# Two wide and narrow matmuls per weight tile become three narrow ones, and the sums are read straight from PSUM

## The chip, the core and the metric

The kernel runs on one core of a Trainium2 chip. TensorE does the matrix products into PSUM, VectorE (DVE), ScalarE (ACT) and GpSimd (POOL) the elementwise work, and the sync engine (SP) issues the loads. The metric is the device time of one execution in microseconds. Before the change it is 2220.55 us, the median of 3 runs that lie between 2220.05 and 2221.08.

## The reference

Two decoder layers over 256 tokens with 2048 features, all in float32. Each layer is a token mixer (latent attention with 8 heads beside retention with 8 heads, both fed by one product with `w_in`) and an MLP with squared ReLU:

```
h = rmsnorm(x, attn_norm[l])
proj = h @ w_in[l]                       # 2048 x 4928
c_q, c_kv, k_rope, rq, rk, rv, rg = jnp.split(proj, split_pts, axis=-1)
a = mla_attention(c_q, c_kv, k_rope, ...)     # w_uq, w_ukv
r = retention(rq, rk, rv, rg, cos128, sin128)
mixed = jnp.concatenate([rmsnorm(a, beta_attn[l]), r * beta_ret[l]], axis=-1)
x = x + mixed @ w_o[l]                   # 2048 x 2048
h = rmsnorm(x, mlp_norm[l])
x = x + jnp.square(jax.nn.relu(h @ w_up[l])) @ w_down[l]   # 2048 x 8192, 8192 x 2048
```

A final rmsnorm follows the last layer.

## The kernel before

**Split operands.** TensorE multiplies float32 data here in the kind float32r. To keep the result near float32, each operand is split into a head of few bits and the exact rest. `split` and `split_w` (L164 to L176) do it: ACT writes the head, DVE subtracts it and writes the rest. A product needs three parts: head by head, head by rest, rest by head.

**One weight tile, two matmuls.** A weight tile is 128 rows by 128 columns. Activations lie features by tokens, as `[128, 2, 256]`: the head's 256 tokens and then the rest's 256. `mac_feat` (L207) issues two matmuls for a weight tile. L209 loads the weight's head and streams all 512 activation columns, head and rest, into a whole PSUM bank. L210 loads the weight's rest and streams the 256 head columns into the bank's first half. So the second half holds one part of the sum and the first half the other two. `mac_tok` (L212) does the same with activations as the loaded side and weights as the streamed side (L214, L215); it serves the retention's values and the latent attention's values.

**The products.** `proj_feat` (L217) computes `nt` products side by side, 128 output features each, over 16 or 32 weight tiles in depth: `nt` is 2 in the token mixer, 4 in the MLP's first product (`UP_TILES`), and 4 or 2 in the output and second MLP products (`OUT_GROUPS`, `END_GROUPS`). Each product owns one of the 8 banks. `stream` (L196) loads 512 KB pieces of weights and splits them, ahead of use, into 6 buffers.

**The joins.** When a product is done, `join` (L225) adds the two halves: ACT copies the second half to SBUF (L227), DVE adds the first half to the copy (L228). `join_scaled` (L230) does so with a scale per token. What follows (squares, gates, ReLU, residual) reads the joined tile. In the MLP's first product it is a DVE operation that squares the ReLU (L643), then the split of the result for the next product.

**The key-value latent.** This product has 320 columns, streamed weights, and the form with three matmuls already (L349 to L351): the loaded tile of L349 and L350 is the same, but each of them loads it.

**Order.** The tile scheduler orders each engine's instructions from the program text, and places semaphore waits. Attention and retention work for the heads is woven between the pieces of the long products (`weave`, L181), in plain float32 matmuls.

Of the kernel before, what the change touches and what calls it, by code (L numbers as in the profile page):

```python
# [15 lines left out]
ALU = mybir.AluOpType  # L16
# [25 lines left out]
def two_pi_parts(scale, *bits):  # L42
    """2 * pi * scale as floats of few bits, whose products with whole numbers are exact, and one with the rest."""
    parts, rest = [], 2 * math.pi
    for n in bits:
        q = 2.0 ** (math.floor(math.log2(rest)) + 1 - n)
        parts.append(math.floor(rest / q) * q * scale)
        rest -= parts[-1] / scale
    return parts + [float(np.float32(rest * scale))]


# An angle is reduced by whole numbers of 2^15 turns, of turns, and of the turns that rounding has left; large parts
# first, while the differences are exact. Per number: turns, then (number, part) to subtract.
# [30 lines left out]
def kernel(ctx: ExitStack, tc: tile.TileContext, xt, positions, w_in, w_uq, w_ukv, w_o, w_up, w_down,  # L84
# [79 lines left out]
    def split(dst, src, scale=None):  # L164
        """dst[:, 0] = 12-bit head of src (times a column), dst[:, 1] = the exact rest."""
        head = dst[:, 0, :]
        if scale is None:
            nc.scalar.copy(head, src)  # L168
            nc.vector.tensor_tensor(dst[:, 1, :], src, head.bitcast(F32), op=ALU.subtract)  # L169
        else:  # L170
            nc.scalar.activation(head, src, AF.Copy, scale=scale)
            nc.vector.scalar_tensor_tensor(dst[:, 1, :], src, scale, head.bitcast(F32), op0=ALU.mult, op1=ALU.subtract)
# [5 lines left out]
    # Work that is woven into the long matrix products, a stage per four k-tiles.  # L178
# [17 lines left out]
    def stream(w, r0, c0, nk, width=256, kc=None):  # L196
        """Yields (k, split tile [P, 2, columns]) for rows r0.. and the columns from c0."""
        kc = kc or 1024 // width
        for s in range(0, nk, kc):
            raw = early.pop(0) if early else w_load(w[r0 + s * P:r0 + (s + kc) * P, c0:c0 + width], [P, kc, width])  # L200
            ws = w_tile([P, kc, 2, width])
            split_w(ws[:, :, 0, :], ws[:, :, 1, :], raw)
            for k in range(kc):
                yield s + k, ws[:, k]
            weave()

    def mac_feat(ps, wk, n0, act, first, last):  # L207
        """Features on partitions: ps[:, :256] + ps[:, 256:] accumulates wk.T @ act."""
        nc.tensor.matmul(ps, wk[:, 0, n0:n0 + P], act.rearrange("p s t -> p (s t)"), start=first, stop=False)  # L209
        nc.tensor.matmul(ps[:, 0:T], wk[:, 1, n0:n0 + P], act[:, 0, :], start=False, stop=last)  # L210

    def mac_tok(ps, wk, t0, act, first, last):  # L212
        """Tokens on partitions: ps[:, :256] + ps[:, 256:] accumulates act.T @ wk."""
        nc.tensor.matmul(ps, act[:, 0, t0:t0 + P], wk, start=first, stop=False)  # L214
        nc.tensor.matmul(ps[:, 0:256], act[:, 1, t0:t0 + P], wk[:, 0], start=False, stop=last)  # L215

    def proj_feat(w, r0, c0, acts, nt=2):  # L217
        ps = [bank() for _ in range(nt)]
        nk = len(acts)
        for k, wk in stream(w, r0, c0, nk, nt * P):  # L220
            for n in range(nt):
                mac_feat(ps[n], wk, n * P, acts[k], k == 0, k == nk - 1)
        return ps

    def join(ps, dst):  # L225
        tb = tmp("tb", 3)
        nc.scalar.copy(tb, ps[:, T:2 * T])  # L227
        nc.vector.tensor_tensor(dst, ps[:, 0:T], tb, op=ALU.add)  # L228

    def join_scaled(ps, dst, col):  # L230
        tb = tmp("tb", 3)
        nc.scalar.activation(tb, ps[:, T:2 * T], AF.Copy, scale=col)
        nc.vector.scalar_tensor_tensor(dst, ps[:, 0:T], col, tb, op0=ALU.mult, op1=ALU.add)

    def rope(ps, dst, cos, sin):
        t = tmp()
        join(ps, t)
        rotate(t, dst, cos, sin)
# [30 lines left out]
    def mean_squares(dst, accs, n, eps):  # L269
        """dst [P, 2] = mean square per token, tokens on partitions, plus eps (a number or a column)."""  # L270
        ps = abank()
        for t in range(2):
            for i, acc in enumerate(accs):
                nc.tensor.matmul(ps[:, t:t + 1], acc[:, t * P:(t + 1) * P], ones, start=i == 0, stop=i == len(accs) - 1)
        if isinstance(eps, float):
            nc.vector.tensor_scalar(dst, ps[:, 0:2], 1.0 / n, eps, op0=ALU.mult, op1=ALU.add)
        else:
            nc.vector.scalar_tensor_tensor(dst, ps[:, 0:2], 1.0 / n, eps, op0=ALU.mult, op1=ALU.add)

    def norm_col(accs, n):  # L280
        """1 / rms per token, tokens on partitions: [P, 2]."""
        v = col("nv")
        mean_squares(v, accs, n, EPS)
        return rsqrt(v, 2)

    def spread(c, tag=None):
        """Tokens from partitions to the free axis, the same on every partition."""
        ps = abank()
        for t in range(2):
            nc.tensor.matmul(ps[:, t * P:(t + 1) * P], c[:, t:t + 1].to_broadcast([P, P]), ident, start=True, stop=True)  # L290
        if tag is None:
            return ps[:, 0:T]
        d = cpool.tile([P, T], F32, tag=tag, name=tag)
        nc.scalar.copy(d, ps[:, 0:T])
        return d
# [5 lines left out]
    def norm_step(acc, tiles, j, g0):  # L301
        """Splits gain * x[j] and adds its squares."""
        xs = xpool.tile([P, 2, T], F32R, tag=f"xs{j}", name=f"xs{j}")
        split(xs, x[j], gcol(g0 + j))
        tiles.append(xs)
        if acc is not None:
            add_square(acc, x[j], j == 0)
# [11 lines left out]
    for l in range(DEPTH):  # L319
        g0 = l * G_LAYER  # L320
        # ================= token mixers =================
        with tc.tile_pool(name=f"mix{l}", bufs=1) as ap:
# [8 lines left out]
            # query latent  # L331
            acc_q = ap.tile([P, T], F32, tag="acccq", name="acccq")
            cq = []
            for c0 in range(COL_CQ, COL_CKV, 256):
                for ps in proj_feat(w_in[l], 0, c0, xs):
                    t = tmp()
                    join(ps, t)
                    add_square(acc_q, t, not cq)
                    s = ap.tile([P, 2, T], F32R, tag=f"cq{len(cq)}", name=f"cq{len(cq)}")
                    split(s, t, gcol(g0 + G_Q + len(cq)))  # L340
                    cq.append(s)

            # key-value latent and shared rotary key, tokens on partitions
# [21 lines left out]
            def scale_rows():  # L365
                # rs for x, and with rmsnorm(rs * c) = c * rsqrt(mean(c * c) + EPS / rs^2) the scales of the latents
# [22 lines left out]
                # feature-major again; the rotary key is kept twice and masked for the two heads of a pair  # L389
# [22 lines left out]
            def mla(i):  # L412
# [15 lines left out]
                for n in range(3):  # L428
                    ps = abank()
                    for k in range(4):  # L430
                        mac_feat(ps, wn[k] if n < 2 else wr[:, k], n * P if n < 2 else 0, cq[k], k == 0, k == 3)
                    if n < 2:
                        join(ps, qn[:, n, :])
                    else:
                        rope(ps, qr, tab[:, 1, 0, :], tab[:, 1, 1, :])
# [6 lines left out]
                for n in range(2):  # L442
                    ps = abank()
                    for k in range(2):
                        mac_feat(ps, wk[:, k], n * 256, ckv[k], k == 0, k == 1)
                    t = tmp()
                    join(ps, t)
                    nc.vector.tensor_tensor(kn[:, n, :], t, rows["tkvb"], op=ALU.mult)
                yield
                wvs = wk.rearrange("p k s (h u c) -> p k s h u c", h=2, u=2)[:, :, :, :, 1, :]  # L450
                for t_ in range(2):
                    ps = abank()
                    for k in range(2):
                        mac_tok(ps, wvs[:, k], t_ * P, ckv[k], k == 0, k == 1)
                    join_scaled(ps, v[:, t_, :], rows["tkv"][:, t_:t_ + 1])
# [51 lines left out]
            def ret_v(i):  # L507
                rv = two("rv")
                ps = [bank(), bank()]
                for k, wk in stream(w_in[l], 0, COL_RV + 256 * i, KD):  # L510
                    for t in range(2):
                        mac_tok(ps[t], wk, t * P, xs[k], k == 0, k == KD - 1)
                for t in range(2):
                    join_scaled(ps[t], rv[:, t, :], rows["rs"][:, t:t + 1])
# [49 lines left out]
            def ret_gate(i, res):  # L564
# [3 lines left out]
                for h, ps in enumerate(pss):  # L568
                    z, th = tmp(), tmp()
                    join(ps, z)  # L570
                    nc.vector.tensor_tensor(z, z, rows["rsb"], op=ALU.mult)
# [41 lines left out]
            for c0, nt in OUT_GROUPS:  # L613
                for n, ps in enumerate(proj_feat(w_o[l], 0, c0 * P, mixed, nt)):
                    j = c0 + n
                    t = tmp()
                    join(ps, t)
                    nc.vector.tensor_tensor(x[j], x[j], t, op=ALU.add)
                    norm_step(acc, ms, j, g0 + G_MLP)

        # ================= MLP =================
        with tc.tile_pool(name=f"mlp{l}", bufs=1) as up:
# [14 lines left out]
            for b in range(FF // FB):  # L637
                us = []
                for c in range(0, FB, UP_TILES * P):
                    for ps in proj_feat(w_up[l], 0, b * FB + c, ms, UP_TILES):  # L640
                        t = tmp()
                        join(ps, t)
                        nc.vector.scalar_tensor_tensor(t, t, 0.0, t, op0=ALU.max, op1=ALU.mult)  # L643
# [4 lines left out]
                for c0, nt in END_GROUPS if end else OUT_GROUPS:  # L648
                    for n, ps in enumerate(proj_feat(w_down[l], b * FB, c0 * P, us, nt)):
                        j = c0 + n  # L650
                        t = tmp()
                        join(ps, t)
                        nc.vector.tensor_tensor(t, t, rows["rs2b"], op=ALU.mult)
# [12 lines left out]
    # ================= final norm =================  # L666
# [36 lines left out]
```

## Time and profile before

| what | value |
|---|---|
| median of 3 runs | 2220.55 us (2220.05 to 2221.08) |
| span of the profiled execution | 2218.1 us |
| outside that span, against the median | 2.45 us |
| TensorE busy | 2191.8 us, 99% of the span |
| weight loads (PEld) busy | 1910.9 us, 86% |
| DVE busy | 1435.0 us, 65% |
| ACT busy | 1075.3 us, 48% |
| HBM traffic | 179 GB/s over the span |

The profiled execution's own time is its span and what lies around it; the median of the runs is 2.45 us longer than the span. Matmuls are pipelined: their lengths overlap, so the time of one is read from the distance between the starts of two neighbours, not from its length. Start times in a timeline are given to 0.01 us.

### The profile page before, as it was taken

The numbers are of one execution on the slowest core, as the hardware profiler recorded it, in microseconds if no ns is written. First come the engines' busy times: TensorE is split into PE (matmuls) and PEld (weight loads), VectorE is DVE, ScalarE is ACT, GpSimd is POOL, SyncE is SP. The second block draws the span as 40 slices with busy tenths as digits, with TensorE's granted clock in tenths as the row PEclk, the third lists the DMA queues.
The fourth block names the chain that finished last, engine by engine and source line by source line (L and its number), as shares of the span: only waits on it lengthen the run. The fifth ranks groups of instructions, "written<-read, shape, count | busy, mean of one in ns | idle before, by whom it ended". The sixth has DMA issues, their size and how long they took to land.

```text
span 2218.1 us, 32536 instructions
## 1 busy us (share of the span) xinstructions
PE 2191.8 (99%) x12552; PEld 1910.9 (86%) x12552; DVE 1435.0 (65%) x2494; ACT 1075.3 (48%) x1655; POOL 24.1 (1%) x34
## 2 busy tenths in 40 slices
PE   7999999999999999999999999999999999999997
PEld 6888888888888888888898888888888888888886
DVE  8878967656554556655668888666565555655564
ACT  7555545444444445444455554555453344444452
POOL 4000000000000000000000000000000000000000
PEclk9999999999999999999999999999999999999998
DMA  7556556666555666555655555566655556665553
GB/s 242 167 157 176 156 187 189 182 189 181 189 182 192 180 193 185 189 185 187 186 170 152 175 164 169 176 191 179 195 182 190 188 184 188 182 189 189 184 178 95
DMA packets 273115, 400.07 MB, mean 180 GB/s; under 512 B 12608, under 2 KB 143808, under 8 KB 272960
## 3 DMA queue, kind: packets, MB, share of 16 engines
q1 hardware_dynamic: 272000, 397.08, 57.9%
q8 instruction: 98, 1.61, 0.3%
q10 hardware_dynamic: 960, 0.92, 0.1%
q14 instruction: 57, 0.47, 0.1%
HBM read 395.85 MB, written 2.10 MB: 179 GB/s over the span
## 4 chain that ended last, share of the span: by engine, by line
PE 98%; DVE 1%; issue 0%; DMA 0%; ACT 0%; SPq 0%; DVEq 0%
PE mm L209 58%; PE mm L210 29%; PE mm L214 3%; PE mm L215 1%; PE at L209 1%; PE at L210 1%; PE at L466 0%; PE at L465 0%; PE mm L351 0%; PE mm L350 0%; PE mm L349 0%; PE at L214 0%; PE at L498 0%; PE at L527 0%; DMA raw<-w_in 0%
## 5 line engine op out<-in xcount | busy, mean ns | idle before, releaser
L176 DVE TENSOR_TENSOR w<-raw,w 128x1024 fp32r<-128x1024 f32 (+3 forms) x792 | 920.0, 1167 | 703.1 <-ACT w L175 702.3
L175 ACT CAST w<-raw 128x1024 fp32r<-128x1024 f32 (+3 forms) x792 | 792.7, 1005 | 919.8 <-PE mm L210 856.0
L209 PE MATMUL mm<-xs,w 128*128 128x512 f32 x2944 | 1048.2, 400 | 7.2 <-ACT w L175 7.2
L210 PE MATMUL mm<-xs,w 128*128 128x256 f32 x2944 | 827.1, 281 | 5.1 <-DVE w L176 5.1
L209 PE MATMUL mm<-u,w 128*128 128x512 f32 x2048 | 723.8, 399 | 0.0
L209 PEld LDWEIGHTS mm<-xs,w 128*128 128x128 f32 x2944 | 554.2, 188 | 141.0 <-ACT w L175 7.2
L210 PE MATMUL mm<-u,w 128*128 128x256 f32 x2048 | 575.3, 281 | 0.0
L210 PEld LDWEIGHTS mm<-xs,w 128*128 128x128 f32 x2944 | 557.4, 189 | 7.8 <-DVE w L176 7.6
L209 PEld LDWEIGHTS mm<-u,w 128*128 128x128 f32 x2048 | 384.9, 188 | 96.0
L210 PEld LDWEIGHTS mm<-u,w 128*128 128x128 f32 x2048 | 387.2, 189 | 0.0
L209 PE MATMUL mm<-mix,w 128*128 128x512 f32 x512 | 181.2, 399 | 0.0
L227 ACT COPY tb<-mm 128x256 f32<-128x256 f32 x280 | 100.6, 372 | 91.4 <-PE mm L210 87.4
L210 PE MATMUL mm<-mix,w 128*128 128x256 f32 x512 | 143.8, 281 | 0.0
L228 DVE TENSOR_TENSOR t<-mm,tb 128x256 f32<-128x256 f32 x280 | 107.9, 416 | 31.7 <-ACT tb L227 31.2
L209 PEld LDWEIGHTS mm<-mix,w 128*128 128x128 f32 x512 | 96.2, 188 | 23.9
L210 PEld LDWEIGHTS mm<-mix,w 128*128 128x128 f32 x512 | 96.8, 189 | 0.0
L214 PE MATMUL mm<-w,xs 128*128 128x512 f32 x256 | 92.5, 402 | 0.0
L215 PE MATMUL mm<-w,xs 128*128 128x256 f32 x256 | 71.5, 279 | 0.0
L168 ACT CAST u<-t 128x256 fp32r<-128x256 f32 x128 | 48.7, 405 | 27.4 <-DVE t L643 27.4
L214 PEld LDWEIGHTS mm<-w,xs 128*128 128x128 f32 x256 | 48.1, 188 | 10.5
L169 DVE TENSOR_TENSOR u<-t,u 128x256 fp32r<-128x256 f32 x128 | 48.9, 422 | 4.6 <-ACT u L168 0.7
L215 PEld LDWEIGHTS mm<-w,xs 128*128 128x128 f32 x256 | 48.3, 189 | 0.0
(167 smaller groups left out, 1102.2 us busy)
## 6 DMA issues: line engine op xcount, KB each, us to landing
raw<-w_up SPq DMA_DIRECT2D x256, 512.0 KB, 4.3
raw<-w_down SPq DMA_DIRECT2D x256, 512.0 KB, 3.7
raw<-w_in SPq DMA_DIRECT2D x144, 512.0 KB, 4.3
raw<-w_o SPq DMA_DIRECT2D x64, 512.0 KB, 4.3
raw<-w_uq SPq DMA_DIRECT2D x16, 384.0 KB, 3.9
raw<-w_in SPq DMA_DIRECT2D x16, 320.0 KB, 3.1
raw<-w_ukv SPq DMA_DIRECT2D x8, 512.0 KB, 4.2
x<-xt SPq DMA_DIRECT2D x8, 256.0 KB, 6.5
```

Source lines behind the costliest of these rows:

```text
L168: nc.scalar.copy(head, src)
L169: nc.vector.tensor_tensor(dst[:, 1, :], src, head.bitcast(F32), op=ALU.subtract)
L175: nc.scalar.copy(dst_h, src)
L176: nc.vector.tensor_tensor(dst_l, src, dst_h.bitcast(F32), op=ALU.subtract)
L209: nc.tensor.matmul(ps, wk[:, 0, n0:n0 + P], act.rearrange("p s t -> p (s t)"), start=first, stop=False)
L210: nc.tensor.matmul(ps[:, 0:T], wk[:, 1, n0:n0 + P], act[:, 0, :], start=False, stop=last)
L214: nc.tensor.matmul(ps, act[:, 0, t0:t0 + P], wk, start=first, stop=False)
L215: nc.tensor.matmul(ps[:, 0:256], act[:, 1, t0:t0 + P], wk[:, 0], start=False, stop=last)
L227: nc.scalar.copy(tb, ps[:, T:2 * T])
L228: nc.vector.tensor_tensor(dst, ps[:, 0:T], tb, op=ALU.add)
```

## The change

Each weight tile gets three matmuls of 256 columns, all into the same 256 columns of PSUM (`three`). Two products share a bank, one in each half (`halves`); only the first matmul of a bank carries the start flag. The sum of the three parts then stands in PSUM, so `join` and `join_scaled` are gone: consumers read PSUM, with a scale where `join_scaled` had one. The MLP's ReLU becomes an ACT operation that reads PSUM, and the square a DVE product of it with the PSUM sum.

```
+    def three(ps, lhs, rhs, start, stop):
+        nc.tensor.matmul(ps, lhs[0], rhs[0], start=start, stop=False, skip_group_check=True)
+        nc.tensor.matmul(ps, lhs[0], rhs[1], start=False, stop=False, skip_group_check=True)
+        nc.tensor.matmul(ps, lhs[1], rhs[0], start=False, stop=stop, skip_group_check=True)
     def mac_feat(ps, wk, n0, act, first, last):
-        nc.tensor.matmul(ps, wk[:, 0, n0:n0 + P], act.rearrange("p s t -> p (s t)"), start=first, stop=False)
-        nc.tensor.matmul(ps[:, 0:T], wk[:, 1, n0:n0 + P], act[:, 0, :], start=False, stop=last)
+        three(ps, [wk[:, s, n0:n0 + P] for s in range(2)], [act[:, s, :] for s in range(2)], first, last)
     def mac_tok(ps, wk, t0, act, first, last):
-        nc.tensor.matmul(ps, act[:, 0, t0:t0 + P], wk, start=first, stop=False)
-        nc.tensor.matmul(ps[:, 0:256], act[:, 1, t0:t0 + P], wk[:, 0], start=False, stop=last)
+        three(ps, [act[:, s, t0:t0 + P] for s in range(2)], [wk[:, s] for s in range(2)], first, last)
+    def halves(n):
+        out = []
+        for i in range(n):
+            if i % 2 == 0:
+                b = bank()
+            out.append(b[:, i % 2 * T:i % 2 * T + T])
+        return out
     def proj_feat(w, r0, c0, acts, nt=2):
-        ps = [bank() for _ in range(nt)]
+        ps = halves(nt)
...
-                mac_feat(ps[n], wk, n * P, acts[k], k == 0, k == nk - 1)
+                mac_feat(ps[n], wk, n * P, acts[k], k == 0 and n % 2 == 0, k == nk - 1)
-    def join(ps, dst):
-        tb = tmp("tb", 3)
-        nc.scalar.copy(tb, ps[:, T:2 * T])
-        nc.vector.tensor_tensor(dst, ps[:, 0:T], tb, op=ALU.add)
...
 -                        join(ps, t)
-                        nc.vector.scalar_tensor_tensor(t, t, 0.0, t, op0=ALU.max, op1=ALU.mult)
+                        nc.scalar.activation(t, ps, AF.Relu)
+                        nc.vector.tensor_tensor(t, t, ps, op=ALU.mult)
...
 -                        join(ps, t)
-                        nc.vector.tensor_tensor(t, t, rows["rs2b"], op=ALU.mult)
+                        nc.vector.tensor_tensor(t, ps, rows["rs2b"], op=ALU.mult)
```

The last two pieces are the MLP's first and second product. The other consumers (query latent, rotary, gate, output product, values) change in the same way.

On TensorE, in the MLP's first product, the eight matmuls of one step in depth for four output tiles stand in a row. `xs15` is the activation tile of that step, `w` the weight piece, `mm` the PSUM bank:

```order
L209 MATMUL mm_4165<-xs15_4154,w_4343 128x512
L210 MATMUL mm_4165<-xs15_4154,w_4343 128x256
L209 MATMUL mm_4166<-xs15_4154,w_4343 128x512
L210 MATMUL mm_4166<-xs15_4154,w_4343 128x256
L209 MATMUL mm_4167<-xs15_4154,w_4343 128x512
L210 MATMUL mm_4167<-xs15_4154,w_4343 128x256
L209 MATMUL mm_4168<-xs15_4154,w_4343 128x512
L210 MATMUL mm_4168<-xs15_4154,w_4343 128x256
```

After the change the same step has twelve matmuls, and two output tiles write to one `mm`:

```order
L210 MATMUL mm_10634<-xs15_4816,w_10841 128x256
L211 MATMUL mm_10634<-xs15_4816,w_10841 128x256
L212 MATMUL mm_10634<-xs15_4816,w_10841 128x256
L210 MATMUL mm_10634<-xs15_4816,w_10841 128x256
L211 MATMUL mm_10634<-xs15_4816,w_10841 128x256
L212 MATMUL mm_10634<-xs15_4816,w_10841 128x256
L210 MATMUL mm_10635<-xs15_4816,w_10841 128x256
L211 MATMUL mm_10635<-xs15_4816,w_10841 128x256
L212 MATMUL mm_10635<-xs15_4816,w_10841 128x256
L210 MATMUL mm_10635<-xs15_4816,w_10841 128x256
L211 MATMUL mm_10635<-xs15_4816,w_10841 128x256
L212 MATMUL mm_10635<-xs15_4816,w_10841 128x256
```

Each L209 of 512 columns has become an L210 and an L211 of 256 columns, each with its own weight load, and the old L210 is now L212; the number of columns stays 768 for a weight tile.

On DVE, at the end of the program, the last two products of the MLP are consumed. `rs2b` is the scale per token, `x_101` the last residual tile, `tb` the copied half, `nv` the start of the final norm:

```order
L228 TENSOR_TENSOR t<-mm,tb 128x256
L653 TENSOR_TENSOR t<-t,rs2b 128x256
L654 TENSOR_TENSOR x_101<-x_101,t 128x256
L253 TENSOR_TENSOR ssq<-ssq,sq 128x256
L228 TENSOR_TENSOR t<-mm,tb 128x256
L653 TENSOR_TENSOR t<-t,rs2b 128x256
L654 TENSOR_TENSOR x_101<-x_101,t 128x256
L276 TENSOR_SCALAR nv<-at 128x2
```

After the change the two additions of the halves are gone and the scaling reads PSUM:

```order
L649 TENSOR_TENSOR t<-mm,rs2b 128x256
L650 TENSOR_TENSOR x_101<-x_101,t 128x256
L257 TENSOR_TENSOR ssq<-ssq,sq 128x256
L649 TENSOR_TENSOR t<-mm,rs2b 128x256
L650 TENSOR_TENSOR x_101<-x_101,t 128x256
L280 TENSOR_SCALAR nv<-at 128x2
```

Nothing else moved there: the last operation before the final norm is still the residual's addition, two instructions (ACT's copy and DVE's addition) earlier in the chain.

## Rows read from the trace of the kernel before

**Rows 1.** The page: span, and busy time with share of each engine

```profile
span 2218.1 us, 32536 instructions
PE 2191.8 (99%) x12552; PEld 1910.9 (86%) x12552; DVE 1435.0 (65%) x2494; ACT 1075.3 (48%) x1655; POOL 24.1 (1%) x34
```

**Rows 2.** The page: lines of the chain that ended last

```profile
PE mm L209 58%; PE mm L210 29%; PE mm L214 3%; PE mm L215 1%; PE at L209 1%; PE at L210 1%; PE at L466 0%; PE at L465 0%; PE mm L351 0%; PE mm L350 0%; PE mm L349 0%; PE at L214 0%; PE at L498 0%; PE at L527 0%; DMA raw<-w_in 0%
```

**Rows 3.** All waits of TensorE: engine, line, releaser; us, times, longest

```profile
PE mm L209 <- ACT w L175: 7.2, 1, 7.2
PE mm L210 <- DVE w L176: 5.1, 4, 2.5
```

**Rows 4.** The page: costliest matmul groups, count, busy us, mean ns

```profile
L209 PE MATMUL mm<-xs,w 128*128 128x512 f32 x2944 | 1048.2, 400 | 7.2 <-ACT w L175 7.2
L209 PE MATMUL mm<-u,w 128*128 128x512 f32 x2048 | 723.8, 399 | 0.0
L209 PE MATMUL mm<-mix,w 128*128 128x512 f32 x512 | 181.2, 399 | 0.0
L214 PE MATMUL mm<-w,xs 128*128 128x512 f32 x256 | 92.5, 402 | 0.0
```

**Rows 5.** Timeline of TensorE in the MLP: start us, length us, instruction

```profile
1000.50 0.28 PE L210 MATMUL mm<-u,w 128*128 128x256 f32 x1
1000.61 0.40 PE L209 MATMUL mm<-u,w 128*128 128x512 f32 x1
...
1001.56 0.28 PE L210 MATMUL mm<-u,w 128*128 128x256 f32 x1
```

**Rows 6.** Stretch of the MLP: length, TensorE busy (instructions), clock, DMA

```profile
600.00:800.00 200.00, 200.00 (x1134) 1.00 0.58 185
```

**Rows 7.** Timeline of TensorE in the first token mixer

```profile
265.22 0.28 PE L210 MATMUL mm<-xs,w 128*128 128x256 f32 x1
265.34 0.39 PE L209 MATMUL mm<-xs,w 128*128 128x512 f32 x1
265.57 0.28 PE L210 MATMUL mm<-xs,w 128*128 128x256 f32 x1
...
266.26 0.28 PE L210 MATMUL mm<-xs,w 128*128 128x256 f32 x1
```

**Rows 8.** Timeline of TensorE in the key-value latent of layer 0

```profile
39.64 0.31 PE L349 MATMUL mm<-w,xs 128*128 128x320 f32 x1
...
47.56 0.31 PE L349 MATMUL mm<-w,xs 128*128 128x320 f32 x1
```

**Rows 9.** Timeline of TensorE: two L210 behind each other, twice

```profile
16.66 0.39 PE L210 MATMUL mm<-xs,w 128*128 128x256 f32 x1
16.89 0.28 PE L210 MATMUL mm<-xs,w 128*128 128x256 f32 x1
...
22.23 0.39 PE L210 MATMUL mm<-xs,w 128*128 128x256 f32 x1 [2.48 <-DVE w L176]
22.46 0.28 PE L210 MATMUL mm<-xs,w 128*128 128x256 f32 x1
```

**Rows 10.** Timeline of TensorE's weight loads there

```profile
22.34 0.19 PEld L210 LDWEIGHTS mm<-xs,w 128*128 128x128 f32 x1
```

**Rows 11.** Timeline of TensorE, two transposes of the latent attention

```profile
107.40 0.38 PE L489 MATMUL at<-cst,pr 128*128 128x128 f32 x2
```

**Rows 12.** TensorE by form, that transpose alone: count, busy us, mean ns

```profile
L489 PE MATMUL at<-cst,pr 128*128 128x128 f32 x48 | 7.9, 273 | 0.0
```

**Rows 13.** Timeline of the last product's consumers

```profile
2202.10 0.37 ACT L227 COPY tb<-mm 128x256 f32<-128x256 f32 x1 [8.57 <-PE mm L210]
...
2202.96 0.42 DVE L653 TENSOR_TENSOR t<-t,rs2b 128x256 f32<-128x256 f32 x1
```

**Rows 14.** The page: the joins' two groups

```profile
L227 ACT COPY tb<-mm 128x256 f32<-128x256 f32 x280 | 100.6, 372 | 91.4 <-PE mm L210 87.4
L228 DVE TENSOR_TENSOR t<-mm,tb 128x256 f32<-128x256 f32 x280 | 107.9, 416 | 31.7 <-ACT tb L227 31.2
```

More of the change, by code (lines that the diff above doesn't have):

```diff
@@ L221, in proj_feat @@
             for n in range(nt):
-                mac_feat(ps[n], wk, n * P, acts[k], k == 0, k == nk - 1)
+                mac_feat(ps[n], wk, n * P, acts[k], k == 0 and n % 2 == 0, k == nk - 1)
         return ps
-    def join(ps, dst):
-        tb = tmp("tb", 3)
-        nc.scalar.copy(tb, ps[:, T:2 * T])
-        nc.vector.tensor_tensor(dst, ps[:, 0:T], tb, op=ALU.add)
[L230 to L233, printed above, removed]
     def rope(ps, dst, cos, sin):
         t = tmp()
-        join(ps, t)
+        nc.scalar.copy(t, ps)
         rotate(t, dst, cos, sin)
@@ L335 @@
                 for ps in proj_feat(w_in[l], 0, c0, xs):
-                    t = tmp()
-                    join(ps, t)
-                    add_square(acc_q, t, not cq)
+                    add_square(acc_q, ps, not cq)
                     s = ap.tile([P, 2, T], F32R, tag=f"cq{len(cq)}", name=f"cq{len(cq)}")
-                    split(s, t, gcol(g0 + G_Q + len(cq)))
+                    split(s, ps, gcol(g0 + G_Q + len(cq)))
                     cq.append(s)
@@ L428, in mla @@
                 for n in range(3):
-                    ps = abank()
+                    ps = abank()[:, 0:T]
                     for k in range(4):
@@ L432, in mla @@
                     if n < 2:
-                        join(ps, qn[:, n, :])
+                        nc.scalar.copy(qn[:, n, :], ps)
                     else:
@@ L442, in mla @@
                 for n in range(2):
-                    ps = abank()
+                    ps = abank()[:, 0:T]
                     for k in range(2):
                         mac_feat(ps, wk[:, k], n * 256, ckv[k], k == 0, k == 1)
-                    t = tmp()
-                    join(ps, t)
-                    nc.vector.tensor_tensor(kn[:, n, :], t, rows["tkvb"], op=ALU.mult)
+                    nc.vector.tensor_tensor(kn[:, n, :], ps, rows["tkvb"], op=ALU.mult)
                 yield
@@ L451, in mla @@
                 for t_ in range(2):
-                    ps = abank()
+                    ps = abank()[:, 0:T]
                     for k in range(2):
                         mac_tok(ps, wvs[:, k], t_ * P, ckv[k], k == 0, k == 1)
-                    join_scaled(ps, v[:, t_, :], rows["tkv"][:, t_:t_ + 1])
+                    nc.scalar.activation(v[:, t_, :], ps, AF.Copy, scale=rows["tkv"][:, t_:t_ + 1])
                 yield
@@ L508, in ret_v @@
                 rv = two("rv")
-                ps = [bank(), bank()]
+                ps = halves(2)
                 for k, wk in stream(w_in[l], 0, COL_RV + 256 * i, KD):
                     for t in range(2):
-                        mac_tok(ps[t], wk, t * P, xs[k], k == 0, k == KD - 1)
+                        mac_tok(ps[t], wk, t * P, xs[k], k == 0 and t == 0, k == KD - 1)
                 for t in range(2):
-                    join_scaled(ps[t], rv[:, t, :], rows["rs"][:, t:t + 1])
+                    nc.scalar.activation(rv[:, t, :], ps[t], AF.Copy, scale=rows["rs"][:, t:t + 1])
                 return rv
@@ L569, in ret_gate @@
                     z, th = tmp(), tmp()
-                    join(ps, z)
-                    nc.vector.tensor_tensor(z, z, rows["rsb"], op=ALU.mult)
+                    nc.vector.tensor_tensor(z, ps, rows["rsb"], op=ALU.mult)
                     nc.scalar.activation(th, z, AF.Tanh, scale=0.5)
@@ L615 @@
                     j = c0 + n
-                    t = tmp()
-                    join(ps, t)
-                    nc.vector.tensor_tensor(x[j], x[j], t, op=ALU.add)
+                    nc.vector.tensor_tensor(x[j], x[j], ps, op=ALU.add)
                     norm_step(acc, ms, j, g0 + G_MLP)
@@ L641 @@
                         t = tmp()
-                        join(ps, t)
-                        nc.vector.scalar_tensor_tensor(t, t, 0.0, t, op0=ALU.max, op1=ALU.mult)
+                        nc.scalar.activation(t, ps, AF.Relu)
+                        nc.vector.tensor_tensor(t, t, ps, op=ALU.mult)
                         u = up.tile([P, 2, T], F32R, tag=f"u{len(us)}", name=f"u{len(us)}")
@@ L651 @@
                         t = tmp()
-                        join(ps, t)
-                        nc.vector.tensor_tensor(t, t, rows["rs2b"], op=ALU.mult)
+                        nc.vector.tensor_tensor(t, ps, rows["rs2b"], op=ALU.mult)
                         nc.vector.tensor_tensor(x[j], x[j], t, op=ALU.add)
```

## The prediction

> **What bounds the kernel now.** I read the page first: TensorE is busy 99% of a span of 2218.1 us, DVE 65%, ACT 48% [rows 1]. The chain of waits confirms that this is the bound: L209 and L210 alone hold 58% and 29% of the span, and L214 and L215 another 4% [rows 2]. The waits of TensorE come next: it waited 7.2 us for the first weights and 5.1 us in four waits for a weight's rest [rows 3], both at the start. So the time is the number of weight tiles times the time of one tile, and any engine but TensorE matters only at the start and at the end.
>
> The number: L209 and L214 have 2944 + 2048 + 512 + 256 = 5760 matmuls [rows 4]; the latent attention adds, by the code, 2 layers x 4 pairs of heads x (3 x 4 + 2 x 2 + 2 x 2) = 160. That is 5920 weight tiles. Of these 4608 lie in the output and MLP products (2 x 256 + 2 x 2048) and 1312 in the token mixers.
>
> The time of one tile now is the distance from an L210 to the next. In the MLP three tiles take 1001.56 - 1000.50 = 1.06 us, 353.3 ns each [rows 5], and a stretch of 200 us holds about 566 tiles at full clock, 353 ns again [rows 6]. There is a second, quicker rhythm in parts of the token mixers: three tiles in 266.26 - 265.22 = 1.04 us, 346.7 ns each [rows 7]. The mixers change between the two; I take 350 ns for them. Streaming 768 columns at the 2.4 GHz level of the clock would be 320 ns, so 27 to 33 ns of a tile are something else. The forecast depends on what.
>
> **The change part by part.**
>
> *The matmuls.* The columns stay 768 per tile, the instructions go from two to three, and the weight loads too: in the key-value latent, which has this form, L350 loads the same tile again. So each of the three costs whatever 256 columns with one load cost. Three places in the trace price that.
>
> First, L210 itself, in its rhythm: 1000.61 - 1000.50 = 0.11 us in the MLP, 265.34 - 265.22 = 0.12 us in the mixer [rows 5, 7]. Subtracting from the tile leaves about 0.235 for the 512 columns, twice as much. Read so, the excess over 2.4 GHz grows with the columns, and a cut costs nothing.
>
> Second, and better, because neighbours of one size share any fault of the time stamps: at two places before the steady stretch two L210 follow each other directly. The ends of the pair are 16.66 + 0.39 = 17.05 and 16.89 + 0.28 = 17.17, then 22.23 + 0.39 = 22.62 and 22.46 + 0.28 = 22.74: 0.12 us apart both times [rows 9]. From the second one's load at 22.34, which I take to begin as the first starts to stream, to the second L210 at 22.46 it is again 0.12 us [rows 9, 10].
>
> Third, the key-value latent: 54 matmuls of 320 columns in 47.56 - 39.64 = 7.92 us, 146.7 ns each [rows 8]. By columns that is 0.458 ns each, or 117.3 ns for 256.
>
> All three give 115 to 120 ns. I take 117, the middle of the first and the third, so 351 ns for a tile. In the 4608 tiles of the output and MLP products that is 353.3 - 351.0 = 2.3 ns less, 10.6 us; in the 1312 of the mixers 1 ns more, 1.3 us. Sum: 9.3 us less.
>
> Bounds: below, the shortest step of load and matmul that the trace has, two transposes in 0.38 us of which one alone is 0.273, so about 0.109 us, with rounding [rows 11, 12], three times that 327 ns. Above, a charge per instruction that has nothing to do with columns: the 320 columns would be 133.3 ns at 2.4 GHz, and 13.3 ns are left [rows 8]; with it 256 columns take 120 ns and a tile 360. The value stands nearer to the row of the same size, L210 behind L210.
>
> *Weight loads.* A load is recorded with 0.19 us, longer than the 0.117 us between matmuls, yet at 22.34 and after it two loads stand closer than that, and each L209 before the change got its load within the one L210 before it [rows 5, 10]. So a load in every 117 ns is something this kernel already does, every second time. That it does so without a break is not shown; the fast step of [rows 11] holds for a few records only.
>
> *The joins.* At least 280 copies on ACT (100.6 us) and 280 additions on DVE (107.9 us) go [rows 14]. The work is hidden behind TensorE except after the last product: there the copy starts at 2202.10 and the scaling at 2202.96 [rows 13], and the scaling can now start where the copy did. That is 0.86 us. In the MLP's first product the copy turns into the ReLU and the addition goes; the squared value comes about one DVE operation sooner, which nothing waits for.
>
> *Banks.* Two products share a bank, so a group of four takes two of eight. TensorE waits for no bank now [rows 3], and less so then. The consumer of the first half may start while the second half gets its last three matmuls; TensorE is past its own wait by then, so this costs nothing.
>
> *The start* waits for loads and splits [rows 3] that the change doesn't touch: nothing.
>
> *Sum.* 2218.1 - 10.6 + 1.3 - 0.9 = 2207.9 us of span, and with the 2.45 us between span and median 2210.4 us. I forecast 2210 us, 0.5% less.
>
> A rule of the skill speaks against this. In the rows 512 columns take about 235 ns, 22 more than 213. The Trainium skill, "TensorE: Matmul & The Clock Gate", section "Wait — 56ns, not 53.3ns?", gives back-to-back matmuls N / 2.4 GHz plus some 2.5 ns each, whatever N is. By it alone the third matmul is an estimated 2.5 ns more per tile, 15 us in all. The trace does not agree on the wide ones, so the sum goes by the rows.
>
> **The rivals.**
>
> *The irregular part stays.* The MLP's 353.3 ns are 6.7 more than the calm rhythm of the mixers [rows 5, 7]. If the calm cost of 256 columns is the 346.7 ns of the tile less the 0.23 us from L209 to L210 there [rows 7], 116.7 ns, and the same 6.7 ns per tile come back in the new form, a tile takes 350 + 6.7 = 356.7 ns: 3.4 more in 4608 tiles and 6.7 more in 1312, 24.5 us. Time: 2220.55 + 24.5 - 0.9 = 2244. For it: the rhythm of the MLP has kept this excess for hundreds of microseconds. Against: L210 there is no longer than in the mixer, so the excess seems to belong to L209. It is slower as soon as a 256-column matmul takes over 118 ns.
>
> *A fixed charge per instruction.* With the 13.3 ns of [rows 8] on each matmul, a tile takes 360 ns: 6.7 x 4608 + 10 x 1312 = 44 us more, 2264 us. For it: the calm tile, 346.7 ns, is 320 and exactly twice 13.3 [rows 7]. Against: by starts L210 is under 120 and the 512 columns over 226.7 in the same rows.
>
> *It cancels out.* At 117.3 ns, the latent's rate, a tile takes 352 ns: 1.3 x 4608 - 2 x 1312 = 3.4 us less, 2216 us. Within 0.2%, which is what a measurement of this kernel can tell from no change, lie tiles of about 351.9 to 353.3 ns.
>
> *The loads turn out the limit, and quick.* If the streaming excess vanished with the short form and only the step of [rows 11] were left, 327 ns per tile would give 2068 us. Nothing but those few records is for it.
>
> **How the numbers follow.** The forecast with its own range of 2200 to 2215 us gets 0.47, the quick loads 0.03; cancelling out 0.17; the irregular part that stays 0.18, the fixed charge 0.15. So faster is 0.50, same 0.17, slower 0.33. The time is that of the likeliest, 2210 us. For 8 in 10 the range reaches over the second rival and short of the full fixed charge: 2198 to 2258 us.
>
> **What would show it.** In the profile after: three matmuls of one tile 351 ns apart from first to first, each 117 from the next, at the stretch of the MLP; about 850 matmuls per 100 us. If they are 120 apart the fixed charge is right, and if they change between 114 and 122 in a pattern the irregular part stayed. The chain should still be TensorE to 98%, with no new wait of TensorE for ACT or DVE; the last product's scaling should follow it by about 0.3 us. A wait for a bank, or TensorE idle behind its own instruction supply, would be a cost that I have left out.

## The result and the profile after

The changed kernel takes 2260.75 us (median of 4 runs, 2260.41 to 2261.46) against 2220.39 us before (4 runs, 2220.05 to 2221.08). The ratio is 1.0182, 95% interval 1.017 to 1.0194: 1.8% slower, where 0.5% faster was forecast, and 2.75 us above the stated range.

The page after, its first lines, the chain by engine and by line, and the three matmul groups of the token mixer and the MLP's first product (columns as in [rows 1, 2, 4]):

```profile
span 2258.8 us, 43807 instructions
PE 2235.3 (99%) x18472; PEld 2230.6 (99%) x18472; DVE 1327.0 (59%) x2142; ACT 1023.2 (45%) x1519; POOL 24.3 (1%) x34
...
PE 98%; DVE 1%; DMA 0%; ACT 0%; issue 0%; SPq 0%; DVEq 0%
PE mm L210 31%; PE mm L212 30%; PE mm L211 30%; PE at L212 1%; PE at L211 1%; PE at L210 1%; PE at L465 0%; PE at L466 0%; PE mm L351 0%; PE mm L353 0%; PE mm L352 0%; PE at L498 0%; PE at L527 0%; DMA raw<-w_in 0%; PE at L489 0%; PE at L294 0%
...
L210 PE MATMUL mm<-xs,w 128*128 128x256 f32 x2944 | 839.6, 285 | 7.3 <-ACT w L175 7.3
L212 PE MATMUL mm<-xs,w 128*128 128x256 f32 x2944 | 834.9, 284 | 3.3 <-DVE w L176 3.3
L211 PE MATMUL mm<-xs,w 128*128 128x256 f32 x2944 | 834.5, 283 | 0.0
```

The bound is where it was: TensorE is busy 99% and holds 98% of the chain, now in three lines of nearly equal share. What is new stands in the same line: weight loads (PEld) are busy 99%, against 86% before [rows 1].

The timeline of TensorE in the MLP, four neighbours:

```profile
1000.51 0.28 PE L212 MATMUL mm<-u,w 128*128 128x256 f32 x1
1000.63 0.28 PE L210 MATMUL mm<-u,w 128*128 128x256 f32 x1
1000.75 0.28 PE L211 MATMUL mm<-u,w 128*128 128x256 f32 x1
1000.87 0.28 PE L212 MATMUL mm<-u,w 128*128 128x256 f32 x1
```

Each starts 0.12 us after the one before, whichever line it is. Three are 0.36 us, where a tile took 0.353 [rows 5]. The token mixer has the same step where the calm rhythm stood before [rows 7]; three tiles of one weight position each, first to first:

```profile
265.18 0.28 PE L210 MATMUL mm<-xs,w 128*128 128x256 f32 x1
...
265.54 0.28 PE L210 MATMUL mm<-xs,w 128*128 128x256 f32 x1
...
265.90 0.28 PE L210 MATMUL mm<-xs,w 128*128 128x256 f32 x1
```

Two tiles in 0.72 us: 360 ns against 346.7. A stretch of the MLP (length, TensorE busy with its instructions, clock, DMA share, GB/s) answers to [rows 6]:

```profile
600.00:800.00 200.00, 200.00 (x1669) 1.00 0.58 184
```

1669 matmuls in 200 us at full clock, 0.12 us each. Neither the irregular rhythm nor a quick one is left in these stretches.

TensorE's waits answer to [rows 3], which calls two lines all of its waits. The view has two more, and so has the kernel before; first after, then the two that are missing of before:

```profile
PE mm L210 <- ACT w L175: 7.3, 1, 7.3
PE mm L212 <- DVE w L176: 3.3, 3, 2.4
PE at L294 <- DVE rs_y L267: 2.4, 1, 2.4
PE at L278 <- ACT sq L656: 1.3, 1, 1.3
```

```profile
PE at L290 <- DVE rs_y L263: 2.5, 1, 2.5
PE at L274 <- ACT sq L660: 2.2, 1, 2.2
```

The waits for weights are at the start and 1.7 us shorter. The two others belong to the final norm, after the last product; the wait for the squares (`sq`) is 0.9 us shorter, which is the shorter way from the last product to its consumers. So between the start and the end no bank, no consumer and no buffer holds TensorE. The end answers to [rows 13]: the last matmul and the scaling of the last product:

```profile
2243.37 0.28 PE L212 MATMUL mm<-u,w 128*128 128x256 f32 x1
...
2243.69 0.42 DVE L649 TENSOR_TENSOR t<-mm,rs2b 128x256 f32<-128x256 f32 x1 [9.73 <-PE mm L212]
```

The scaling starts 0.32 us after the last matmul does, without the 0.86 us of copy and addition.

The sum of the loss: 6.7 ns in 4608 tiles are 30.7 us, and 0.86 us at the end and 1.7 us of waits go the other way. The span grew by 2258.8 - 2218.1 = 40.7 us, which leaves 12.6 us for the 1312 tiles of the token mixers, 9.6 ns each: from about 350 to 360. The second mixer taken alone, from its first matmul with `w_in` to the first with `w_o`, says the same: it lasts from 1109.44 to 1386.95 us before and from 1129.15 to 1413.10 us after, 6.4 us longer for 656 tiles.

### The profile page after: what moved, and what is told of

The parts are those of the page before. It is cut to its first block, busy times and chain, and to the rows that moved or that the text cites. A ratio compares the mean times of both kernels' runs of the same rounds, so it can differ in the third digit from the quotient of the medians.

```text
span 2258.8 us, 43807 instructions
## 1 busy us (share of the span) xinstructions
PE 2235.3 (99%) x18472; PEld 2230.6 (99%) x18472; DVE 1327.0 (59%) x2142; ACT 1023.2 (45%) x1519; POOL 24.3 (1%) x34
## 4 chain that ended last, share of the span: by engine, by line
PE 98%; DVE 1%; DMA 0%; ACT 0%; issue 0%; SPq 0%; DVEq 0%
PE mm L210 31%; PE mm L212 30%; PE mm L211 30%; PE at L212 1%; PE at L211 1%; PE at L210 1%; PE at L465 0%; PE at L466 0%; PE mm L351 0%; PE mm L353 0%; PE mm L352 0%; PE at L498 0%; PE at L527 0%; DMA raw<-w_in 0%; PE at L489 0%; PE at L294 0%
## 5 line engine op out<-in xcount | busy, mean ns | idle before, releaser
L210 PE MATMUL mm<-xs,w 128*128 128x256 f32 x2944 | 839.6, 285 | 7.3 <-ACT w L175 7.3
L212 PE MATMUL mm<-xs,w 128*128 128x256 f32 x2944 | 834.9, 284 | 3.3 <-DVE w L176 3.3
L211 PE MATMUL mm<-xs,w 128*128 128x256 f32 x2944 | 834.5, 283 | 0.0
L210 PE MATMUL mm<-u,w 128*128 128x256 f32 x2048 | 579.6, 283 | 0.0
L211 PE MATMUL mm<-u,w 128*128 128x256 f32 x2048 | 579.6, 283 | 0.0
L212 PE MATMUL mm<-u,w 128*128 128x256 f32 x2048 | 579.6, 283 | 0.0
L210 PEld LDWEIGHTS mm<-xs,w 128*128 128x128 f32 x2944 | 566.5, 192 | 7.5 <-ACT w L175 7.3
L212 PEld LDWEIGHTS mm<-xs,w 128*128 128x128 f32 x2944 | 566.4, 192 | 4.0 <-DVE w L176 4.0
L211 PEld LDWEIGHTS mm<-xs,w 128*128 128x128 f32 x2944 | 566.6, 192 | 0.2
L210 PEld LDWEIGHTS mm<-u,w 128*128 128x128 f32 x2048 | 393.2, 192 | 0.0
L211 PEld LDWEIGHTS mm<-u,w 128*128 128x128 f32 x2048 | 393.2, 192 | 0.0
L212 PEld LDWEIGHTS mm<-u,w 128*128 128x128 f32 x2048 | 393.2, 192 | 0.0
L210 PE MATMUL mm<-mix,w 128*128 128x256 f32 x512 | 145.0, 283 | 0.0
L212 PE MATMUL mm<-mix,w 128*128 128x256 f32 x512 | 144.9, 283 | 0.0
L211 PE MATMUL mm<-mix,w 128*128 128x256 f32 x512 | 144.9, 283 | 0.0
L210 PEld LDWEIGHTS mm<-mix,w 128*128 128x128 f32 x512 | 98.3, 192 | 0.0
L211 PEld LDWEIGHTS mm<-mix,w 128*128 128x128 f32 x512 | 98.3, 192 | 0.0
L212 PEld LDWEIGHTS mm<-mix,w 128*128 128x128 f32 x512 | 98.3, 192 | 0.0
L210 PE MATMUL mm<-w,xs 128*128 128x256 f32 x256 | 74.0, 289 | 0.0
L212 PE MATMUL mm<-w,xs 128*128 128x256 f32 x256 | 72.4, 283 | 0.0
```

The costliest lines, as they stand in the source:

```text
L210: nc.tensor.matmul(ps, lhs[0], rhs[0], start=start, stop=False, skip_group_check=True)
L211: nc.tensor.matmul(ps, lhs[0], rhs[1], start=False, stop=False, skip_group_check=True)
L212: nc.tensor.matmul(ps, lhs[1], rhs[0], start=False, stop=stop, skip_group_check=True)
```

## The experiments

The question was what the 120 ns are. 256 columns at 2.4 GHz are 106.7 ns. The other 13.3 could be a fixed charge of every matmul of this kind (A), the pace of the weight loads (B), something that grows with the columns, or the cost of adding onto columns just written or of loading one tile twice. The first four kernels ran once each, without an interval, beside a run of the kernel before at 2220.07 us.

**Fewer columns.** From the changed kernel:

```
+NARROW = 192
...
+        if not first:
+            ps, rhs = ps[:, 0:NARROW], [r[:, 0:NARROW] for r in rhs]
         nc.tensor.matmul(ps, lhs[0], rhs[0], start=start, stop=False, skip_group_check=True)
...
```

> The changed kernel with 64 of the 256 token columns left out of each feature-major matmul of the long products from the second step in depth on (192 columns streamed instead of 256; so the sums of those tokens are incomplete). In the changed kernel every matmul starts exactly 120 ns after the one before. Theory A, a fixed 13.3 ns per instruction on top of the columns at 2.4 GHz: 192 / 2.4 + 13.3 = 93.3 ns a step, some 1830 us. Theory B, the weight load sets the pace and the columns are hidden behind it: the step stays 120 ns, time near 2260 us. Theory C, both: the step stops at the 107 to 109 ns that stand between two loads elsewhere in the trace, some 2080 us.

2137.98 us. The timeline of TensorE in the MLP, and a stretch of it:

```profile
900.81 0.27 PE L213 MATMUL mm<-u,w 128*128 128x192 f32 x1
900.92 0.27 PE L214 MATMUL mm<-u,w 128*128 128x192 f32 x1
...
901.48 0.28 PE L213 MATMUL mm<-u,w 128*128 128x192 f32 x1
```

```profile
600.00:700.00 100.00, 100.00 (x897) 1.00 0.60 196
```

Six steps in 901.48 - 900.81 = 0.67 us, 111.7 ns; 897 matmuls in 100 us say the same. The fixed charge would have given 93.3, the loads as the pace of the 120 would have left 120. Neither happened alone: the step stops in between, as in C, whose own numbers, 107 to 109 ns and 2080 us, were too low by some 3 to 5 ns and 58 us. There is a floor of about 111 ns for these matmuls, and the 120 ns lie above it, so the floor is not what sets them. Whether it is the pace of the loads was not tested.

**Wide ones only.** From the kernel before:

```
-        nc.tensor.matmul(ps, wk[:, 0, n0:n0 + P], act.rearrange("p s t -> p (s t)"), start=first, stop=False)
-        nc.tensor.matmul(ps[:, 0:T], wk[:, 1, n0:n0 + P], act[:, 0, :], start=False, stop=last)
+        nc.tensor.matmul(ps, wk[:, 0, n0:n0 + P], act.rearrange("p s t -> p (s t)"), start=first, stop=last)
```

> The kernel before with L210 left out in the feature-major products (weight's rest by activation's head is missing), so that only matmuls of 512 columns follow each other. Theory A (fixed 13.3 ns): 213.3 + 13.3 = 226.7 ns a step, some 1510 us. Theory by columns (0.46 ns a column): 235 to 236 ns, some 1560 us. Theory B (load) gives nothing to wait for here: 213 to 216 ns, some 1440 us. DVE and ACT, which split the weights, may set the time in the token mixers; the step in the MLP decides.

1628.59 us, above all three forecasts; DVE and ACT hold TensorE up, in the mixers above all, as feared, so the step decides. The timeline merges eleven of the same line in the MLP:

```profile
599.62 2.65 PE L209 MATMUL mm<-xs,w 128*128 128x512 f32 x11
```

The last one's own length is 0.39 us, so ten steps take 2.65 - 0.39 = 2.26 us: 226 ns. That is 213.3 + 13.3, not 235. With equal neighbours the excess is the same 13.3 ns at 256, at 320 [rows 8] and at 512 columns. It does not grow with the columns, and at 226 ns from one load to the next a floor near 111 ns can't be its cause.

**Two-byte operands.** From the changed kernel, with the heads read without the bitcast:

```
-F32R = mybir.dt.float32r
+F32R = mybir.dt.bfloat16
...
```

> The changed kernel with all split operands in bfloat16 instead of float32r (less exact; same instructions, columns and weight loads). If the 13.3 ns belong to 4-byte operands (their load or their stream), the step falls to about 109 ns and the time to some 2065 us. If they belong to every matmul with a load of its own, the step stays 120 ns and the time near 2260 us.

2067.74 us. The timelines of TensorE and of its weight loads:

```profile
899.83 0.27 PE L211 MATMUL mm<-u,w 128*128 128x256 bf16 x1
...
900.93 0.27 PE L212 MATMUL mm<-u,w 128*128 128x256 bf16 x1
```

```profile
900.05 0.10 PEld L211 LDWEIGHTS <-w 128*128 128x128 bf16 x1
```

Ten steps in 1.10 us, 0.11 us, and the load's length is 0.10 instead of 0.19 us. The time gives it more finely: 2260.75 - 2067.74 = 193 us over the 17760 matmuls of the weight tiles are some 10.9 ns each, 109 ns a step. So most of the 13.3 ns belong to operands of 4 bytes. The Trainium skill, "TensorE: Matmul & The Clock Gate", section "Wait — 56ns, not 53.3ns?", gives back-to-back matmuls N / 2.4 GHz and some 2.5 ns, for 256 columns an estimated 109.2 ns: the trace agrees for bfloat16, and does not for float32r, where 120 is measured. Which side carries the charge, the loaded or the streamed operand, stays open: a kernel with only one of the two in 2 bytes was not run, and neither was one whose matmuls share a load.

**Part by part.** From the changed kernel, over the output tiles of a step in depth:

```
-            for n in range(nt):
-                mac_feat(ps[n], wk, n * P, acts[k], k == 0 and n % 2 == 0, k == nk - 1)
+            for i, (a, b) in enumerate(((0, 0), (0, 1), (1, 0))):
+                for n in range(nt):
+                    nc.tensor.matmul(ps[n], wk[:, a, n * P:n * P + P], acts[k][:, b, :],
+                                     start=k == 0 and i == 0 and n % 2 == 0, stop=k == nk - 1 and i == 2, skip_group_check=True)
```

> The changed kernel with the three parts of a step in depth issued part by part over the two or four output tiles, so that two neighbouring matmuls no longer add to the same 256 PSUM columns and no tile is loaded twice in a row. If adding onto the columns just written, or reloading the same tile, costs the 13.3 ns, the step falls towards 107 to 110 ns and the time to 2030 to 2090 us. Theories A and B: 120 ns as before, 2260 us.

2260.30 us, within 0.5 us of the changed kernel. Nine matmuls of the MLP, merged:

```profile
1000.20 1.24 PE L237 MATMUL mm<-u,w 128*128 128x256 f32 x9
```

(1.24 - 0.28) / 8 = 0.12 us. Neither adding onto columns just written nor loading one tile twice in a row costs anything.

**The cut alone.** From the kernel before, joins, banks and token-major products as they were:

```
-        nc.tensor.matmul(ps, wk[:, 0, n0:n0 + P], act.rearrange("p s t -> p (s t)"), start=first, stop=False)
+        for s in range(2):
+            nc.tensor.matmul(ps[:, s * T:(s + 1) * T], wk[:, 0, n0:n0 + P], act[:, s, :], start=first and s == 0, stop=False, skip_group_check=True)
...
```

> The kernel before with one part of the change alone: in the feature-major products L209's 512 columns are cut into two matmuls of 256 that write the two halves of the bank as before; joins, one product to a bank and the token-major products (288 of the 5920 weight tiles) stay. If the cut is the whole loss, a tile takes 3 x 120 = 360 ns: 6.7 ns more in 4608 tiles and some 10 more in 1024, 41 us more, 2261 us. If shared banks or the new consumers carry a good part of the loss, it comes out nearer to 2220 us.

2260.35 us (4 runs) against 2220.25 (7 runs), ratio 1.018, interval 1.0163 to 1.0197. TensorE in the MLP, from one rest matmul to the next:

```profile
1000.09 0.28 PE L211 MATMUL mm<-u,w 128*128 128x256 f32 x1
1000.21 0.40 PE L210 MATMUL mm<-u,w 128*128 128x256 f32 x2
1000.45 0.28 PE L211 MATMUL mm<-u,w 128*128 128x256 f32 x1
```

0.36 us a tile again. The cut is the whole loss: this kernel and the changed one are 0.4 us apart. Between them stand the removed joins, the shared banks and the new consumers, which gain the 0.9 us at the end, and the cut in the 288 token-major tiles, which costs an estimated 2.9 us at some 10 ns each. So the removed work is worth 2 to 3 us at most, although in the changed kernel DVE is busy 108 us less and ACT 52 us less than before [rows 1].

**Equal neighbours.** If a matmul's price is fixed when its neighbours are equal, the 353.3 ns of the MLP before are 6.7 too many for 226.7 + 120. Four kernels keep the two matmuls of before and only reorder them, all wide ones of a group first; the group is one step in depth, one weight piece, two pieces or four. The reordering, for a group of pieces:

```
+            for i, wi in held:
+                for n in range(nt):
+                    nc.tensor.matmul(ps[n], wi[:, 0, n * P:n * P + P], acts[i].rearrange("p s t -> p (s t)"), start=i == 0, stop=False)
+            for i, wi in held:
+                for n in range(nt):
+                    nc.tensor.matmul(ps[n][:, 0:T], wi[:, 1, n * P:n * P + P], acts[i][:, 0, :], start=False, stop=i == nk - 1)
...
```

> The kernel before, with the matmuls of a step in depth reordered in the feature-major products: first the 512-column ones of all two or four output tiles, then their 256-column ones. Same instructions, same columns. Fixed charge without irregularity: 226.7 and 120 ns, 346.7 a tile, against 353.3 in the MLP: 31 us less there and some 4 in the mixers, 2186 us. If a change of size costs something each time, two changes in a step of four tiles are left of eight: 2190 to 2200 us. If the 6.7 ns have another cause: 2220 us.

> As the kernel with the wide matmuls first, but over a whole weight piece (8 output tile and depth pairs): eight 512-column matmuls, then eight 256-column ones. If each change of size costs, this is quicker than the grouping by step, by 2 to 6 us; if the rhythm is calm in both, the same within 2 us. Narrow matmuls of a piece wait for the weight's rest together, which is split after the head: if the split comes late, TensorE waits less at the start.

By step 2206.71 us, ratio 0.9938 (0.9923 to 0.9953); by piece 2200.95 us, ratio 0.9913 (0.9898 to 0.9928). The stretch of the MLP, by step and then by piece:

```profile
600.00:800.00 200.00, 200.00 (x1143) 1.00 0.57 187
```

```profile
600.00:800.00 200.00, 200.00 (x1148) 1.00 0.58 189
```

Two matmuls a tile: less the two or so that began before the stretch, the counts give about 350.5 and 349 ns a tile, from 353.3. The gain is there, but the calm 346.7 is not reached; both numbers for the order by step, 2186 and 2190 to 2200 us, were too good. By piece is 5.8 us quicker than by step, as expected if each change of size costs. Where the rest is, the merged timeline by piece shows:

```profile
1001.44 2.00 PE L227 MATMUL mm<-u,w 128*128 128x512 f32 x8
1003.28 1.12 PE L230 MATMUL mm<-u,w 128*128 128x256 f32 x8
1004.23 0.40 PE L227 MATMUL mm<-u,w 128*128 128x512 f32 x1
```

Eight wide ones take 1.84 us, 230 ns each, eight narrow ones 0.95 us, 119. Start by start the wide ones have some 27 ns too many in eight and the narrow ones a few too few. The round as a whole is sharper if many are taken together; two starts of a wide group, 49 rounds apart:

```profile
602.00 2.00 PE L227 MATMUL mm<-u,w 128*128 128x512 f32 x8
...
738.87 2.00 PE L227 MATMUL mm<-u,w 128*128 128x512 f32 x8
```

136.87 / 49 = 2.793 us a round, 349.2 ns a tile, and eight calm tiles are 2.773: 20 ns a round. The kernel by step, at 350.5 a tile, has about 15 in its round of four. So it looks like a price per round, and the round was made longer.

> As the kernel with the wide matmuls first over a whole weight piece, but over two pieces (16 wide, then 16 narrow; half as many changes of size). A round of wide and narrow takes 20 ns over 226.7 and 120 each in the kernel of one piece, so 1.25 ns a tile are left instead of 2.5: 347.9 ns a tile, some 7 us less than 2201 us, 2194 us. If the changes of size are not the cause, 2201 us.

> As above over four pieces (32 wide, then 32 narrow): 0.6 ns a tile are left, some 3.5 us less than with two, 2190 us, unless four of the six buffers for split weights are held so long that the next piece comes late: then TensorE waits for ACT or DVE, and it is slower than with two pieces.

With two pieces 2204.36 us, ratio 0.9929 (0.9915 to 0.9943); with four 2237.89 us, ratio 1.0076 (1.0063 to 1.0089). Both forecasts of the whole were missed, though the second named waits as what could undo it. In the MLP the mechanism held with two pieces: 16 wide ones in 4.19 - 0.54 = 3.65 us, 228 ns each, and 1151 matmuls in 200 us:

```profile
1000.54 3.82 PE L228 MATMUL mm<-u,w 128*128 128x512 f32 x16
1004.19 1.59 PE L231 MATMUL mm<-u,w 128*128 128x256 f32 x12
```

```profile
600.00:800.00 200.00, 200.00 (x1151) 1.00 0.57 187
```

Taken over many rounds, 24 of them from 605.30 to 738.90 us last 5.567 us each, 20 ns over 16 calm tiles, and with four pieces 11 rounds from 607.76 to 730.01 us last 11.114 us each, again 20 ns over. From eight tiles on the price of a round is the same. It is not for shorter rounds: a round of one tile costs 6.7 ns in the MLP before and nothing in the calm rhythm.

The loss is in waits. Some of TensorE's with two pieces, then with four:

```profile
PE at L551 <- DVE rv L243: 4.6, 4, 1.6
```

```profile
PE at L499 <- DVE pr L492: 12.7, 10, 2.7
PE mm L228 <- ACT w L176: 10.1, 4, 7.3
PE at L284 <- DVE ssq L263: 9.4, 2, 4.7
```

L551 (retention's output) waits for values that DVE makes; with four pieces the transposes of the attention (L499), the split weights (L228; 7.3 us of them are the start) and the norms (L284) wait too. The values themselves are no slower: DVE starts on them 4.1 us after the last matmul of their product, by piece and with two pieces alike. What has moved is the work in front of L551 (L550 in the kernel by piece). TensorE by piece, then with two pieces:

```profile
163.63 1.99 PE L227 MATMUL mm<-xs,w 128*128 128x512 f32 x8
165.45 1.12 PE L230 MATMUL mm<-xs,w 128*128 128x256 f32 x8
...
167.81 0.38 PE L550 MATMUL at<-rv,sT 128*128 128x128 f32 x2
```

```profile
165.39 0.28 PE L211 MATMUL at<-cq,w 128*128 128x256 f32 x1
167.24 0.46 PE L551 MATMUL at<-rv,sT 128*128 128x128 f32 x2 [1.57 <-DVE rv L243]
```

By piece the matmuls of a weight piece fill the time until DVE is done. With two pieces the first piece's matmuls are held until the second has come, the work of the heads that is woven in between goes first, and nothing fills the time before it. All waits of TensorE are 15.6 us by piece, 21.2 with two pieces and 46.6 with four. With four the granted clock of the span is 0.990, against 0.997 by piece: after the wait of 4.7 us that ends at 405 us, for one, it is 0.50, the 1.2 GHz level, from 406 to 408.5 us. The 5.6 us of waits with two pieces are not all of the some 9 us lost outside the MLP and the output product; the rest was not traced.

So: one piece in the token mixers, two in the output and MLP products.

```
-    def proj_feat(w, r0, c0, acts, nt=2):
+    def proj_feat(w, r0, c0, acts, nt=2, pieces=1):
...
+        group, held = pieces * 1024 // (nt * P), []
...
-                for n, ps in enumerate(proj_feat(w_o[l], 0, c0 * P, mixed, nt)):
+                for n, ps in enumerate(proj_feat(w_o[l], 0, c0 * P, mixed, nt, 2)):
...
```

> The wide-first order over one weight piece in the token mixers (where the grouping by two pieces made TensorE wait for DVE) and over two pieces in the output and MLP products (where it did not). From the kernel of one piece, 2201 us: 1.25 ns less in 4608 tiles, 5.8 us, so 2195 us. If the two-piece grouping loses elsewhere too: 2201 us or more.

2195.44 us (4 runs) against 2220.14 (7 runs), ratio 0.9889, interval 0.9873 to 0.9906. All waits of TensorE in it:

```profile
PE mm L227 <- ACT w L175: 7.8, 2, 7.3
PE mm L227 <- DVE xs L172: 3.6, 2, 2.4
PE at L299 <- DVE rs_y L272: 2.5, 1, 2.5
PE at L283 <- ACT sq L669: 2.2, 1, 2.2
```

The expected 2195 us came, and none of the waits of TensorE for the heads' work is left. This is the best kernel of the study: 1.1% under the kernel before and 65 us under the changed one.

## Why the prediction was wrong

**The step that failed** is the price of a 256-column matmul with a load of its own, "I take 117". It is 120.0 ns, and 5920 tiles x 3 x 3 ns are 53 us: with 120 the same sum gives 2264 us, 3 us from the measured time. The count of tiles, the columns, the unchanged bound, the end (0.86 us) and the absence of new waits were right.

Why 117 came out: two of the three readings were wrong in kind, not only in size.

- The distance from L210 to the next L209 [rows 5, 7] was read as L210's price. Neighbours there have different sizes. With equal ones the prices are 120 (after) and 226 (wide only), which add up to the calm tile's 346.7 [rows 7] within 1 ns; the starts had split the same sum into about 117 and 230. The sum of a period was sound, its split by starts was not.
- The latent's 146.7 ns were scaled by columns to 117.3 [rows 8]. Subtracting the columns at 2.4 GHz leaves 13.3, and that is what carries over to 256 and 512 columns.
- The two L210 in a row [rows 9, 10] gave 0.12 us both times, which reads like the answer. That is luck: the reading goes by the ends, which the profile models, while the starts of each pair lie 0.23 us apart, and at 0.01 us it can't tell 120 from 117. The middle of the first reading, 115, and the third, 117.3, would have been 116; 117 was a choice.

**"A fixed charge per instruction"** was the right rival, with 2264 us for 2260.75. Its reason "the calm tile is 320 and exactly twice 13.3" was the strongest evidence on the page: two streams of different make-up, one constant, no remainder. The reason against it rested on the split by starts. It got 0.15, and the range was cut short of it. The sign that the prediction named for it, matmuls 120 ns apart, is what came.

**"The irregular part stays"** fell: the steps after are 120 ns throughout the MLP. The irregular rhythm was seen only with unequal neighbours; the kernel with only wide matmuls does not show it, and longer groups of equals shrink it. Why two sizes in turn run calmly in parts of the mixers and irregularly in the MLP was not settled.

**"The loads turn out the limit"** fell as a gain: with 256 columns the step is 120 ns, not the 109 of [rows 11]. A floor exists, at 111 ns with 192 columns, but below the 120; whether the loads are its cause was not tested.

**The rule of the Trainium skill** ("TensorE: Matmul & The Clock Gate", section "Wait — 56ns, not 53.3ns?"), some 2.5 ns for each matmul, had the right sign, with an estimated 15 us where 40 were lost. For float32r the runs give 13.3 ns a matmul.

## What to carry to other kernels

When matmuls are cut or merged, price them by a stretch of equal matmuls, or by the whole period of a pattern; subtract the columns' time first and see whether one constant fits several sizes. Work that is hidden behind a full engine (here 160 us of it) is worth next to nothing when removed, while a matmul added on that engine cost its 13.3 ns here, less what the calmer rhythm gave back. On a bound engine the order alone can be worth something: equal matmuls behind each other gave 1.1% here, as long as the order did not take away the matmuls behind which other engines' work was hidden.

## What the hardware showed that was not expected

- Matmuls in float32r with a load each, equal neighbours at full clock: 120 ns for 256 columns, 146.7 for 320, 226 for 512, that is the columns at 2.4 GHz and 13.3 ns; 192 columns take about 111 ns, where the same sum would be 93.3. In bfloat16 256 columns take 109 ns.
- A round of eight, sixteen or thirty-two wide matmuls and as many narrow ones takes 20 ns more than the sum of their own prices. It shows where the wide ones begin: eight take 1.84 us instead of 1.81, sixteen 3.65 instead of 3.63.
